# Four of the eight up chunks of three MLP rounds by seven products instead of eight

## The chip, the cores and the metric

The kernel runs on one core of a Trainium2 chip. The metric is the time of one execution on the device in microseconds (us). The kernel before was run three times: 1208.88 us in the median, 1205.19 the lowest and 1209.29 the highest. One further execution was recorded by the profiler, and everything that is read from the trace is from that one.

## What is computed

One inference step of two decoder layers, for a prompt of 512 tokens and eight samples of 8 tokens each, which share all weights: 576 tokens with 1024 features. Layer 0 mixes by retention and gated spatial mixing, layer 1 by windowed attention. After each mixer stands the MLP, and the MLP's first half is what the change touches:

```python
def sqrelu_mlp(h, w_up, w_down):
    return jnp.square(jax.nn.relu(h @ w_up)) @ w_down

hp = hp + sqrelu_mlp(rmsnorm(hp, norm_mlp[l]), mlp_w_up[l], mlp_w_down[l])
```

Here `h` has 1024 features, the hidden layer 4096. All is fp32. The kernel keeps that precision by splitting each operand of a product into a high part that the matrix engine takes in one pass (type fp32r) and the rest, the low part, and by adding three products: high by high, high by low, low by high.

## The kernel before

**Layout.** Activations lie with features on the 128 partitions and tokens along the free side. The residual is eight tiles `h[0]` to `h[7]` of 128 x 576. A matmul takes 288 tokens, one half of them. The normalised input of an MLP is eight pairs of tiles, `norm.xs[k]` = (high, low); the factor 1/rms (`norm.rv`) is multiplied in after the product.

**Rounds.** The hidden layer is worked off in four rounds of 1024 hidden features (`rounds_of`, `FB` = 8 chunks of 128 features a round). Each round has an up stage and a down stage.

The up stage runs four pairs of chunks. `up()` makes a chunk: 8 input blocks x 3 products x 2 token halves = 48 matmuls into two PSUM banks, the tile `acc`. VectorE then evacuates it, relu times 1/rms, into `t` (line 496), and ScalarE squares `t` into a quarter of the tile `q` (line 501). After both chunks of a pair, `combine` (lines 533 to 536, four VectorE operations of 288 columns) forms four sums and differences in `q`, and `two` splits seven blocks of `q` into the high tile `ahi` (ScalarE, line 504) and the low tile `alo` (VectorE, line 505), first three blocks (864 columns), then four (1152). `q` has one buffer.

The down stage multiplies these by the down weights, and it already works by seven products for eight (the scheme of Strassen and Winograd for 2 x 2 blocks: a pair of output chunks, two token halves, pairs of hidden chunks). `down_unit` does one of four such units in a round: products P1 to P7 of 12 matmuls each into PSUM banks (`product`, line 346), ScalarE copies of partial results from one bank to the next (`y`, `z`, `w`), and VectorE adding the results to `h` (line 557). The first unit of a round runs P1, P2, P3 and P5 for three of its four block rows first and then the fourth row of each, since the fourth needs the last pair of the up stage.

**Weights.** `order` lists all weight blocks of 512 KB in the order of use, and `jobs` the pieces in which they are split. An ordinary chunk has two pieces, `left` and `right`, of 512 columns; a unit has seven, of which four are of sums (`s1` to `s4`, VectorE, line 263, 512 columns each). `load_to` (line 235) issues the loads on SP's queue into `raw`, which has three buffers; the second weight of down units 1 and 3 is loaded into the place of `q` instead (the list `spare`). `prepare` and `split_low` split a piece: ScalarE casts the high part (line 278), VectorE subtracts it (line 289). High and low parts have six buffers each (`NW_`), so a piece can be split at most some five products ahead of its use.

**The order of work.** Inside `mlp`, VectorE and ScalarE take their instructions in the order in which the program writes them (`tc.manual_schedule`). `ahead_to(n)` writes the sums, casts and splits of the coming pieces at that place; it stands after every product and every chunk, ahead of the operations that evacuate that product's result. `raw` of a chunk comes free with the split of its `right` piece, of a unit's two weights with P2 and with P4.

## Time and profile before

| | us | share of the span |
|---|---|---|
| profiled execution | 1204.73 | |
| its span, first to last instruction | 1202.9 | 100% |
| TensorE matmul (PE) busy, 9130 instructions | 1182.9 | 98% |
| TensorE weight load (PEld) busy | 1164.8 | 97% |
| VectorE (DVE) busy, 1691 instructions | 908.2 | 76% |
| ScalarE (ACT) busy, 1111 instructions | 588.4 | 49% |
| GpSimd (POOL) busy | 148.3 | 12% |
| DMA, mean of the 16 engines | 91 GB/s | |

The granted TensorE clock is 0.997 of full speed over the span. A row of a timeline gives start, duration, engine, line, operation, what it writes and reads, and in brackets how long the engine stood idle before it and what ended that. Durations of neighbouring instructions overlap a little; the distance from start to start is what a queued instruction takes of its engine. In names, `t<-acc` writes `t` and reads `acc`.

### The profile page before, as it was taken

Reading aid. Unit: us, or ns where it says so; the run is one execution under the profiler, and the core shown is the slowest. Engines: PE = TensorE matmul, PEld = TensorE weight load, DVE = VectorE, ACT = ScalarE, POOL = GpSimd, SP = SyncE. Lnnn points to the kernel's source line nnn. Section 1 sums busy time; section 2 is a strip of 40 time slices with the busy share of each in tenths; the row PEclk is TensorE's granted clock in tenths of the full one; section 3 lists DMA queues with packets and bytes.
Section 4 is the critical chain, followed back from the end, with each engine's and each line's share of the span. In section 5 each row is a group of like instructions: output and inputs, shape, how many; then the busy total and the mean of one; then the engine's idle time right before and its main releaser. Section 6 shows DMA issues by size and latency. Waiting matters only on the chain.

```text
span 1202.9 us, 22619 instructions
## 1 busy us (share of the span) xinstructions
PE 1182.9 (98%) x9130; PEld 1164.8 (97%) x9130; DVE 908.2 (76%) x1691; ACT 588.4 (49%) x1111; POOL 148.3 (12%) x130
## 2 busy tenths in 40 slices
PE   8999999999999999999999999999999999999996
PEld 8899999999999999999999998999999999999996
DVE  8977797987866876885797787546785795795696
ACT  6333554654534444443466877445453453453452
POOL 4444250000000000000002653220000000000000
PEclk9999999999999999999999999999999999999999
DMA  7343222322332232242223211122233233233322
GB/s 269 110 142 112 88 65 80 88 81 78 90 106 87 77 117 71 71 120 75 88 87 111 72 53 55 53 76 71 84 105 89 71 106 91 68 106 88 87 73 79
DMA packets 38264, 109.43 MB, mean 91 GB/s; under 512 B 4160, under 2 KB 12544, under 8 KB 38144
## 3 DMA queue, kind: packets, MB, share of 16 engines
q1 hardware_dynamic: 37440, 107.36, 29.1%
q8 instruction: 72, 1.18, 0.4%
q10 hardware_dynamic: 720, 0.62, 0.2%
q14 instruction: 32, 0.26, 0.1%
HBM read 102.92 MB, written 6.03 MB: 91 GB/s over the span
## 4 chain that ended last, share of the span: by engine, by line
PE 82%; DVE 10%; ACT 4%; DMA 3%; issue 1%; SPq 0%; DVEq 0%; ACTq 0%
PE acc L334 50%; PE acc L346 10%; PE y L346 4%; PE f L346 4%; PE w L346 3%; PE z L346 3%; DVE wlo L289 3%; DMA raw<-in_w_dn 2%; ACT s L1158 1%; DVE alo L505 1%; PE tpp L1218 1%; DVE h L557 1%; ACT ahi L504 1%; PE dn L334 1%; PE op L1233 1%
## 5 line engine op out<-in xcount | busy, mean ns | idle before, releaser
L334 PE MATMUL acc<-xhi,whi 128*128 128x288 f32 x1504 | 321.7, 295 | 0.3 <-DVE vz L809 0.3
L334 PE MATMUL acc<-xhi,wlo 128*128 128x288 f32 x1504 | 319.2, 293 | 0.0
L334 PE MATMUL acc<-xlo,whi 128*128 128x288 f32 x1504 | 318.6, 293 | 0.0
L289 DVE TENSOR_TENSOR wlo<-raw,whi 128x512 fp32r<-128x512 f32 x317 | 235.7, 757 | 68.8 <-ACT whi L278 67.5
L334 PEld LDWEIGHTS acc<-xhi,whi 128*128 128x128 f32 x1504 | 239.5, 188 | 1.6 <-issue 1.1
L334 PEld LDWEIGHTS acc<-xhi,wlo 128*128 128x128 f32 x1504 | 240.5, 188 | 0.3
L334 PEld LDWEIGHTS acc<-xlo,whi 128*128 128x128 f32 x1504 | 240.1, 188 | 0.0
L278 ACT CAST whi<-raw 128x512 fp32r<-128x512 f32 x317 | 188.9, 619 | 100.5 <-PE acc L334 73.3
L501 ACT ACTIVATE q<-t 128x576 f32<-128x576 f32 x64 | 44.0, 687 | 227.8 <-DVE t L496 227.8
L278 ACT CAST whi<-s 128x512 fp32r<-128x512 f32 x140 | 83.4, 621 | 72.4 <-DVE s L263 62.8
L496 DVE SCALAR_TENSOR_TENSOR t<-acc,rstd 128x576 f32<-128x576 f32 x64 | 48.3, 755 | 80.6 <-PE acc L334 80.4
L289 DVE TENSOR_TENSOR wlo<-s,whi 128x512 fp32r<-128x512 f32 x140 | 95.9, 697 | 10.8 <-ACT whi L278 10.8
L505 DVE TENSOR_TENSOR alo<-q,ahi 128x864 fp32r<-128x864 f32 x64 | 77.2, 1205 | 8.3 <-ACT ahi L504 8.3
L504 ACT CAST ahi<-q 128x864 fp32r<-128x864 f32 x64 | 66.6, 1041 | 13.5 <-DVE q L536 12.5
L346 PE MATMUL acc<-ahi,wlo 128*128 128x288 f32 x340 | 71.4, 298 | 0.6
L346 PE MATMUL acc<-ahi,whi 128*128 128x288 f32 x340 | 71.4, 295 | 0.0
L346 PE MATMUL acc<-alo,whi 128*128 128x288 f32 x340 | 70.4, 295 | 0.0
L1102 POOL TENSOR_TENSOR kl<-z,kh 64x512 fp32r<-64x512 f32 x4 | 5.5, 1374 | 475.1 <-ACT kh L1099 474.9
L263 DVE TENSOR_TENSOR s<-raw 128x512 f32<-128x512 f32 x70 | 48.7, 695 | 19.8 <-DMA raw<-in_w_dn 19.8
L346 PEld LDWEIGHTS acc<-ahi,wlo 128*128 128x128 f32 x340 | 53.5, 188 | 2.5 <-DVE wlo L289 2.5
L346 PEld LDWEIGHTS acc<-ahi,whi 128*128 128x128 f32 x340 | 54.0, 188 | 0.0
L346 PEld LDWEIGHTS acc<-alo,whi 128*128 128x128 f32 x340 | 53.7, 188 | 0.0
(386 smaller groups left out, 2118.8 us busy)
## 6 DMA issues: line engine op xcount, KB each, us to landing
raw<-in_w_up SPq DMA_DIRECT2D x64, 512.0 KB
raw<-in_w_dn SPq DMA_DIRECT2D x64, 512.0 KB
raw<-in_w_in SPq DMA_DIRECT2D x22, 512.0 KB
raw<-in_w_o SPq DMA_DIRECT2D x16, 512.0 KB
raw<-in_w_qkv SPq DMA_DIRECT2D x10, 512.0 KB
h<-in_xT SPq DMA_DIRECT2D x8, 288.0 KB
s<-in_s SPq DMA_DIRECT2D x4, 512.0 KB
out_ret_s<-s SPq DMA_DIRECT2D x4, 512.0 KB
```

Of the source, the lines that this page charges most:

```text
L263: nc.vector.tensor_tensor(out=sums[k, i], in0=x, in1=b[y], op=ALU.add)
L278: nc.scalar.copy(out=hi, in_=src)
L289: nc.vector.tensor_tensor(out=lo, in0=src, in1=hi.bitcast(F32), op=ALU.subtract)
L334: nc.tensor.matmul(out, lhsT=w_, rhs=x_[:, hf if isinstance(hf, slice) else half(hf)], start=(start and si == 0), stop=(stop and si == 2))
L346: nc.tensor.matmul(out, lhsT=w[wi][:, k * P:(k + 1) * P], rhs=x(k)[xi], start=(start and n == 0), stop=(stop and n == len(steps) - 1), ski ...
L496: nc.vector.scalar_tensor_tensor(out=halves(t), in0=view, scalar=0.0, in1=norm.rv, op0=ALU.max, op1=ALU.mult)
L501: nc.scalar.activation(out=flat(q[:, seg]), in_=t, func=AF.Square)
L504: nc.scalar.copy(out=hi[:, s0 - 1:s1 - 1], in_=q[:, s0:s1])
L505: nc.vector.tensor_tensor(out=lo[:, s0 - 1:s1 - 1], in0=q[:, s0:s1], in1=hi.bitcast(F32)[:, s0 - 1:s1 - 1], op=ALU.subtract)
L557: nc.vector.tensor_tensor(out=row[:, cols_], in0=row[:, cols_], in1=src, op=op)
L1158: nc.scalar.activation(out=s[:, n, cut_:], in_=s[:, n, cut_:], func=AF.Exp, bias=nm[:, n:n + 1], accum_out=den[:, n:n + 1])
L1218: nc.tensor.transpose(out=tp[:, i * P:(i + 1) * P], in_=s[:, n, hf * P:(hf + 1) * P], identity=ident)
```

## The change

In rounds 1, 2 and 3 of each MLP, pairs 1 and 3 of the up chunks become a unit of seven products as in the down stage (`up_unit`). The 2 x 2 blocks are two hidden chunks, two token halves, and pairs of input blocks. The four mixed operands of the input (`mixed`, split in high and low) are made once, by `mix`, in round 0, which keeps its eight plain chunks. The result of each product chain stands in a bank of its own (`x`, `y`, `f`, `z`, `w`); ScalarE copies `x` to `y`, `x` to `z` and `z` to `w`, each ahead of the product that goes on in the copy, and `f` into `q`. VectorE adds `f` to `z` and to `x`, and scales each of the four quarters (relu, or minimum with 0 where the sign is turned, times 1/rms); ScalarE squares two quarters at a time.

The combination and split of a pair (`pending`) move: where a unit follows, to behind its P1 and the copy of `y`; elsewhere to the start of the next pair, and for the last pair of a round to the end of the up stage. The plain chunks write their evacuation straight into `q` and square it there, and take their input blocks in the order 0, 2, 4, 1, 3, 5, 6, 7. The up weights are laid out on the host so that a block of 512 KB holds the same numbers in the order that both uses share; there are as many loads of the same size. A scratch size for DMA is set to 4096 bytes.

```diff
--- before.py
+++ after.py
@@ -113,6 +113,7 @@
 NCOL = 59
 UNIT = ("P1", "P5", "P6", "P2", "P7", "P3", "P4")
 SUMS = {"P1": "s1", "P5": "s2", "P2": "s3", "P6": "s4"}
+MIX = ((0, 1), (1, 0), (2, 0), (3, 0))
 FIRST_UNIT = ("P1", "P2", "P3", "P5", "P6", "P4", "P7")
 
 
@@ -200,10 +201,19 @@
             if m % 2:
                 spare.append(len(order) - 1)
 
+    def in_units(r, p):
+
+        return r > 0 and p % 2 == 1
+
     def mlp_order(l, last):
         up, dn = a[f"w_up{l}"], a[f"w_dn{l}"]
         for r in range(32 // FB):
-            add_pieces([up[r * FB + f] for f in range(FB)])
+            for p in range(FB // 2):
+                pair = [up[r * FB // 2 + p, i] for i in range(2)]
+                if in_units(r, p):
+                    add_unit(pair, False)
+                else:
+                    add_pieces(pair)
             for m in range(KC // 2):
                 if last and r == 32 // FB - 1 and m == KC // 2 - 1:
                     add_pieces([dn[r, m, i] for i in range(2)])
@@ -469,52 +479,138 @@
 
     def rounds_of(norm, nxt, mp):
         rounds, closing = 32 // FB, Closing(COL["fin"])
+        operand = {"P1": 0, "P2": 2, "P3": 1, "P5": 3, "P6": 4, "P7": 5, "P4": 6}
+        mixed = []
 
         def up():
 
             acc, got = acc_tile(), take(2)
-            for k in range(KC):
-                block([acc[:, hf, 0:TH] for hf in range(2)], cut(got, k), norm.xs[k], (0, 1), k == 0, k == KC - 1)
+            for n, k in enumerate((0, 1, 2, 4, 5, 6, 3, 7)):
+
+                block([acc[:, hf, 0:TH] for hf in range(2)], cut(got, k), norm.xs[2 * (k % 4) + k // 4], (0, 1),
+                      n == 0, n == KC - 1)
             ahead_to(used[0] + NW_ - 2)
             return acc[:, :, 0:TH]
 
+        def mix(i, q):
+
+            a, b = 2 * i, 2 * i + 1
+            ga, gb = (cols[:, norm.gcol + c:norm.gcol + c + 1] for c in (a, b))
+            one, two_ = slice(TH, T), slice(0, TH)
+            t1, t3, u2, u4 = (q[:, n] for n in range(4, 8))
+            nc.scalar.activation(out=t3, in_=h[a][:, two_], func=AF.Copy, scale=ga)
+            for out, src, g, in1, op in ((t1, h[a][:, one], ga, t3, ALU.subtract), (t3, h[b][:, two_], gb, t3, ALU.subtract),
+                                         (u2, h[b][:, two_], gb, t1, ALU.add), (u4, h[b][:, one], gb, u2, ALU.subtract)):
+                nc.vector.scalar_tensor_tensor(out=out, in0=src, scalar=g, in1=in1, op0=ALU.mult, op1=op)
+            his, los = [], []
+            for src, sign in ((q[:, 4:6], 1.0), (q[:, 6:8], -1.0)):
+                hi, lo = (ks("xn", F32R) if i % 2 else mp.tile([P, T], F32R, name="xn", tag="xn", bufs=8) for _ in range(2))
+                nc.scalar.activation(out=halves(hi), in_=src, func=AF.Copy, scale=sign)
+                nc.vector.scalar_tensor_tensor(out=halves(lo), in0=src, scalar=sign, in1=halves(hi.bitcast(F32)),
+                                               op0=ALU.mult, op1=ALU.subtract)
+                for mine, t in ((his, hi), (los, lo)):
+                    mine.extend(halves(t)[:, n] for n in range(2))
+            his, los = ([v[n] for n in (0, 2, 1, 3)] for v in (his, los))
+            parts_ = []
+            for part, mine in zip(range(2), (his, los)):
+                xa, xb = norm.xs[a][part], norm.xs[b][part]
+                parts_.append([xa[:, one], xb[:, two_], xb[:, one]] + mine)
+            mixed.append(parts_)
+
+        def up_unit(last_pair):
+
+            x = acc_tile()[:, 0, 0:TH]
+
+            def run(n, out, start, ahead=NW_ - 1):
+                product(out, take(1)[0], lambda k: [t[operand[n]] for t in mixed[k]], range(4), start, True, True)
+                if ahead:
+                    ahead_to(used[0] + ahead)
+
+            def copied(name, src):
+                out = m_tile(name)[:, 0:TH]
+                nc.scalar.copy(out=out, in_=src)
+                ahead_to(used[0] + NW_ - 1)
+                return out
+
+            def scaled(seg, src, op):
+                nc.vector.scalar_tensor_tensor(out=q[:, seg], in0=src, scalar=0.0, in1=norm.rv[:, seg % 2],
+                                               op0=op, op1=ALU.mult)
+
+            run("P1", x, True, 0)
+            y = m_tile("y")[:, 0:TH]
+            nc.scalar.copy(out=y, in_=x)
+            last_pair()
+            q = q_tile()
+            ahead_to(used[0] + NW_ - 1)
+            f = m_tile("f")[:, 0:TH]
+            run("P5", f, True)
+            run("P6", x, False, 0)
+            z = copied("z", x)
+
+            nc.scalar.copy(out=q[:, 3], in_=f)
+            run("P2", y, False)
+            scaled(1, y, ALU.max)
+            run("P7", z, False, 0)
+            w_ = copied("w", z)
+
+            nc.vector.tensor_tensor(out=q[:, 2], in0=z, in1=q[:, 3], op=ALU.add)
+            scaled(2, q[:, 2], ALU.min)
+            run("P3", x, False)
+            nc.vector.tensor_tensor(out=q[:, 0], in0=x, in1=q[:, 3], op=ALU.add)
+            scaled(0, q[:, 0], ALU.max)
+            nc.scalar.activation(out=flat(q[:, 0:2]), in_=flat(q[:, 0:2]), func=AF.Square)
+            run("P4", w_, False)
+            scaled(3, w_, ALU.min)
+            nc.scalar.activation(out=flat(q[:, 2:4]), in_=flat(q[:, 2:4]), func=AF.Square)
+            return q
+
+        def q_tile():
+
+            return mp.tile([P, 8, TH], F32, name="q", tag="q", bufs=1)
+
         def flat(v):
             return v.rearrange("p a b -> p (a b)")
 
+        pending = lambda: None
         for r in range(rounds):
             acts, firsts = [], []
             for p in range(FB // 2):
-
-                q = mp.tile([P, 8, TH], F32, name="q", tag="q", bufs=1)
-                hi = mp.tile([P, 7, TH], F32R, name="ahi", tag="ahi", bufs=FB // 2)
-                lo = mp.tile([P, 7, TH], F32R, name="alo", tag="alo", bufs=FB // 2)
-                for j in range(2):
+                if in_units(r, p):
+                    q = up_unit(pending)
+                else:
+                    pending()
+                    q = q_tile()
+                for j in range(0 if in_units(r, p) else 2):
                     view = up()
                     if r == 0 and p == 0 and j == 0:
                         norm.finish()
-                    t = mp.tile([P, T], F32, name="t", tag="t")
-                    nc.vector.scalar_tensor_tensor(out=halves(t), in0=view, scalar=0.0, in1=norm.rv,
+                    seg = slice(2 * j, 2 * j + 2)
+                    nc.vector.scalar_tensor_tensor(out=q[:, seg], in0=view, scalar=0.0, in1=norm.rv,
                                                    op0=ALU.max, op1=ALU.mult)
                     if p == FB // 2 - 1 and j == 1:
                         ahead_to(used[0] + NW_ - 1)
-                    seg = slice(2 * j, 2 * j + 2)
-                    nc.scalar.activation(out=flat(q[:, seg]), in_=t, func=AF.Square)
-
-                def two(s0, s1):
-                    nc.scalar.copy(out=hi[:, s0 - 1:s1 - 1], in_=q[:, s0:s1])
-                    nc.vector.tensor_tensor(out=lo[:, s0 - 1:s1 - 1], in0=q[:, s0:s1],
-                                            in1=hi.bitcast(F32)[:, s0 - 1:s1 - 1], op=ALU.subtract)
-
-                b12 = q[:, 0]
-                combine(*(q[:, i] for i in range(8)))
-                two(1, 4)
-                two(4, 8)
-                acts.append([[t_[:, i] for i in range(7)] for t_ in (hi, lo)])
-                if nxt is None and r == rounds - 1:
-
-                    bh, bl = (mp.tile([P, TH], F32R, name=n, tag=n, bufs=FB // 2) for n in ("b12h", "b12l"))
-                    split_into(b12, bh, bl)
-                    firsts.append((bh, bl))
+                    nc.scalar.activation(out=flat(q[:, seg]), in_=flat(q[:, seg]), func=AF.Square)
+                    if r == 0 and (p, j) in MIX:
+                        mix(MIX.index((p, j)), q)
+
+                def pending(q=q, acts=acts, firsts=firsts, r=r):
+
+                    hi = mp.tile([P, 7, TH], F32R, name="ahi", tag="ahi", bufs=FB // 2)
+                    lo = mp.tile([P, 7, TH], F32R, name="alo", tag="alo", bufs=FB // 2)
+                    combine(*(q[:, i] for i in range(8)))
+                    for seg in (slice(0, 3), slice(3, 7)):
+                        src = q[:, seg.start + 1:seg.stop + 1]
+                        nc.scalar.copy(out=hi[:, seg], in_=src)
+                        nc.vector.tensor_tensor(out=lo[:, seg], in0=src, in1=hi.bitcast(F32)[:, seg], op=ALU.subtract)
+                    acts.append([[t_[:, i] for i in range(7)] for t_ in (hi, lo)])
+                    if nxt is None and r == rounds - 1:
+
+                        bh, bl = (mp.tile([P, TH], F32R, name=n, tag=n, bufs=FB // 2) for n in ("b12h", "b12l"))
+                        split_into(q[:, 0], bh, bl)
+                        firsts.append((bh, bl))
+
+            pending()
+            pending = lambda: None
             between = []
             spare_open[0] = True
             for m in range(KC // 2):
@@ -1412,6 +1508,10 @@
         r = len(w) // D
         return w.reshape(r, 4, 2, P, 4, 2, P).transpose(0, 4, 5, 3, 2, 1, 6).reshape(r, 4, 2, P, 8, P)
 
+    def up(w):
+
+        return w.reshape(4, 2, P, 16, 2, P).transpose(3, 4, 2, 1, 0, 5).reshape(16, 2, P, 8, P)
+
     def cols(v):
         return v.reshape(-1, P).T
 
@@ -1447,14 +1547,14 @@
         "rot": ROT,
     }
     for l in range(2):
-        out[f"w_up{l}"] = chunks(i["mlp_w_up"][l])
+        out[f"w_up{l}"] = up(i["mlp_w_up"][l])
         out[f"w_dn{l}"] = down(i["mlp_w_down"][l])
     return {k: np.ascontiguousarray(v) for k, v in out.items()}
 
 
 def kernel(**inputs):
     arrays = layouts({k: np.asarray(v) for k, v in inputs.items()})
-    nc = bacc.Bacc("TRN2", target_bir_lowering=False, num_devices=1)
+    nc = bacc.Bacc("TRN2", target_bir_lowering=False, num_devices=1, dynamic_dma_scratch_size=4096)
     a = {k: nc.dram_tensor("in_" + k, v.shape, F32, kind="ExternalInput").ap() for k, v in arrays.items()}
     o = {k: nc.dram_tensor("out_" + k, s, F32, kind="ExternalOutput").ap() for k, s in OUTS.items()}
     with tile.TileContext(nc) as tc:
```

## The prediction

> **What bounds the kernel now.** I read the page's first part, then a table by stage, then the chain of waits that ended last, then the VectorE, ScalarE and TensorE timelines around the end of one round.
>
> ```profile
> span 1202.9 us, 22619 instructions
> PE 1182.9 (98%) x9130; PEld 1164.8 (97%) x9130; DVE 908.2 (76%) x1691; ACT 588.4 (49%) x1111; POOL 148.3 (12%) x130
> ```
>
> TensorE (PE) is busy nearly all the time. That is an average, so the next view takes one round of the first MLP apart: its up stage, then its down stage.
>
> ```profile
> 350.00:400.00 50.00, 50.00 (x387) 50.00 (x386) 29.26 (x46) 19.47 (x29) 0.00 (x0) 1.00 0.27 83
> 400.00:445.00 45.00, 44.92 (x337) 44.49 (x336) 39.61 (x74) 22.90 (x42) 0.00 (x0) 1.00 0.34 96
> ```
>
> The columns after the stretch are its length, then PE, weight loads, VectorE (DVE), ScalarE (ACT), GpSimd. PE is full in both stages at granted clock 1.00. DVE is 59% busy in the up stage and 88% in the down stage: the up stage has the spare DVE time, and there the change works.
>
> ```profile
> 350.01 49.93 PE acc L334 x384
> 405.62 3.51 DMA raw<-in_w_dn
> 414.80 1.59 PE acc L346 x12
> 416.39 1.60 PE y L346 x12
> ...
> 445.05 49.93 PE acc L334 x384
> ```
>
> These rows of the chain give PE's prices. An up stage of 8 chunks is 384 matmuls in 49.93 us, so a pair of chunks (96) takes 12.48 us. A product of a down unit (12 matmuls) takes 1.593 us (414.80 to 416.39), a round 95.0 (350.01 to 445.05). The DMA row shows that each round hangs on something besides PE: a weight load issued at 405.62. The next fence is DVE from the last two pairs of this up stage into the down stage.
>
> ```profile
> 387.49 0.76 DVE L496 SCALAR_TENSOR_TENSOR t<-acc,rstd 128x576 f32<-128x576 f32 x1 [1.07 <-PE acc L334]
> 388.16 0.45 DVE L533 TENSOR_TENSOR q<-q 128x288 f32<-128x288 f32 x1
> 389.00 0.46 DVE L534 SCALAR_TENSOR_TENSOR q<-q 128x288 f32<-128x288 f32 x1 [0.39 <-ACT q L501]
> ...
> 391.42 1.36 DVE L505 TENSOR_TENSOR alo<-q,ahi 128x1152 fp32r<-128x1152 f32 x1 [0.26 <-ACT ahi L504]
> 392.70 0.69 DVE L263 TENSOR_TENSOR s<-raw 128x512 f32<-128x512 f32 x1
> 393.30 1.29 DVE L289 TENSOR_TENSOR wlo<-raw,whi 128x512 fp32r<-128x512 f32 x2
> 394.50 1.41 DVE L263 TENSOR_TENSOR s<-s,raw 128x512 f32<-128x512 f32 x2
> 395.83 0.75 DVE L496 SCALAR_TENSOR_TENSOR t<-acc,rstd 128x576 f32<-128x576 f32 x1
> 397.91 1.29 DVE L289 TENSOR_TENSOR wlo<-s,whi 128x512 fp32r<-128x512 f32 x2 [1.32 <-ACT whi L278]
> 399.97 0.76 DVE L496 SCALAR_TENSOR_TENSOR t<-acc,rstd 128x576 f32<-128x576 f32 x1 [0.77 <-PE acc L334]
> 400.64 0.68 DVE L289 TENSOR_TENSOR wlo<-s,whi 128x512 fp32r<-128x512 f32 x1
> ...
> 402.17 0.45 DVE L535 TENSOR_TENSOR q<-q 128x288 f32<-128x288 f32 x1
> 402.54 0.46 DVE L536 SCALAR_TENSOR_TENSOR q<-q 128x288 f32<-128x288 f32 x1
> ...
> 404.23 1.36 DVE L505 TENSOR_TENSOR alo<-q,ahi 128x1152 fp32r<-128x1152 f32 x1 [0.27 <-ACT ahi L504]
> ...
> 409.15 0.69 DVE L263 TENSOR_TENSOR s<-raw 128x512 f32<-128x512 f32 x1 [1.43 <-DMA raw<-in_w_dn]
> ```
>
> Three things are to be seen. First, DVE works in program order: the evacuation at 395.83 comes with no idle time before it, behind sums and splits. Second, the round's last combination and split end at 405.59 (404.23 + 1.36). PE begins the down stage at 399.77 and reaches the matmul that needs them at 405.87:
>
> ```profile
> 399.77 0.55 PE L346 MATMUL acc<-ahi,whi 128*128 128x288 f32 x3
> 405.87 0.29 PE L346 MATMUL f<-alo,whi 128*128 128x288 f32 x1
> ```
>
> So the cover is 0.28 us. Third, that same end frees the buffer q, in which the second weight of down unit 1 lands (issue 405.62), and DVE stands still for it until 409.15, 3.53 us after the issue. The chain from the last up evacuation through this split and this load is therefore as long as PE's own work: whatever comes later at 405.59 makes the round later by as much.
>
> **The change, part by part.** *Products.* In rounds 1 to 3 pairs 1 and 3 become units of seven products: 7 x 1.593 = 11.15 us for 12.48, so 1.33 us less PE work in each of 12 units, 15.9 us in all.
>
> *DVE work of a unit.* Start-to-start distances are the price of queued instructions: 0.60 us for 512 columns (392.70 to 393.30), 0.67 for an evacuation of 576 (387.49 to 388.16), 0.37 for 288 (402.17 to 402.54). A pair of chunks has 4 splits and 2 evacuations: 3.74 us. A unit has 7 splits, 4 sums and 6 instructions of 288 (four scalings, two additions): 11 x 0.60 + 6 x 0.37 = 8.82. Combination and split of the activations are common to both. So DVE gains 5.1 us of work a unit, while PE gives it 1.33 us less time. The four operations of 288 that read PSUM are not in the trace as such; between half of the 576 row (0.34) and a 288 row (0.37) I take the latter.
>
> [...]
>
> *The end of a round.* The second unit (pair 3) must be followed at once by the down stage. I count DVE's queue from the evacuation of the chunk before the pair (387.49) to the end of the last split (405.59): 18.10 us now. Afterwards:
> - that evacuation, combination and split of pair 2: 387.49 to 392.70, 5.21 us, as now;
> - eight splits of weights (P7, P3, P4 of the unit and five ahead for the down stage; the six weight buffers allow none earlier) and the four sums for down unit 0: 12 x 0.60 = 7.2;
> - six operations of 288: 2.2;
> - a new wait. After P3 ScalarE squares two halves, then casts the weight for P6 of the down unit, and that weight's split stands in DVE's queue ahead of the scaling of P4's result. DVE waits out the square and the cast, 1.3 us by the rows below (0.69 + 0.62). Queued behind it are the scaling, the combination and both splits;
> - from the second square to the end of the split as now: 388.28 to 392.78, 4.50, and 0.1 before it.
>
> Sum 20.5 us, 2.4 more than now. ScalarE's rows for this are:
>
> ```profile
> 388.28 0.69 ACT L501 ACTIVATE q<-t 128x576 f32<-128x576 f32 x1 [4.29 <-DVE t L496]
> ...
> 397.27 1.65 ACT L278 CAST whi<-s 128x512 fp32r<-128x512 f32 x3
> ...
> 405.14 0.38 ACT L573 COPY acc<-acc 128x288 f32<-128x288 f32 x1 [0.94 <-PE acc L346]
> 405.43 0.62 ACT L278 CAST whi<-raw 128x512 fp32r<-128x512 f32 x1
> ```
>
> *Late entry.* The unit of pair 1 loads DVE the same way: 5.21, eight splits, two sums, six of 288 and the wait. Its first sum for pair 3 needs that unit's second weight. There are three buffers, so this load cannot be issued before the second half of pair 2's first weight is split, 5.2 + 5 x 0.60 = 8.2 us after the evacuation that precedes unit 1; it lands 3.5 later, at 11.7. DVE asks at 8.2 + 0.60 + 3 x 0.37 = 9.9 and waits up to 1.8. From there its chain ends as that of unit 3: 11.7 + 0.6 (sum) + 0.6 (split) + 0.74 + 1.3 + 0.6 + 0.37 + 4.6 = 20.5. Pair 2 still asks DVE for a sum, a split and an evacuation (22.4), then ScalarE for a square and two casts (0.69 + 2 x 0.55) and DVE for the last split: 24.8. PE's end of pair 2 asks for the next evacuation at 11.15 + 12.48 = 23.6. So unit 3 would begin 1.2 us late; without the wait of 1.8 it begins on time. Between 0 and 1.2, the difference of two sums of twenty rows, I take the middle, 0.6.
>
> *What stays covered.* ScalarE's four new copies (0.29 each by 405.14 to 405.43), among them z ahead of P7: it is queued behind both activation casts and three weight casts, so it ends about 5.9 us into the unit, and P7 begins at 6.4. With the late entry, P7 of the second unit waits 0.1 to 0.7; this lies in DVE's shadow and adds nothing to the chain above. Nothing is added to SP's queue: as many loads of 512 KB as before, in the same order; the smaller scratch and the new block order in the chunks remove and add no instruction, and I cost them at 0.
>
> *Per round.* Gain of the first unit 1.33 (PE is not held there); the second unit's gain is lost, since DVE's chain ends later than PE. So +2.4 + 0.6 - 1.33 = +1.7 us, with ends +1.1 and +2.3. Six rounds: +10 (6.5 to 14).
>
> *Round 0.* It keeps its chunks and gains four mixes. One mix is four DVE operations of 288 and two of 576, 4 x 0.37 + 2 x 0.67 = 2.8, with waits for ScalarE's square, copy and casts of some 1.1. The last lies between the evacuations at 395.83 and 399.97, where DVE idles 1.32 + 0.77 = 2.1. About 1.8 sticks out if none of the waits overlap, 0 if they fall into the idle time; I take 0.9 in each MLP, 2 us in all.
>
> **Sum.** The profiled execution took 1204.73 us (span 1202.9 and 1.8 around it): +12 gives 1217. It lies 4.2 under the median of the three runs, 1208.88, and 0.5 under the lowest, 1205.19; I add half of the first, 2, and say 1219.
>
> **Rivals.** *The gain arrives (faster).* PE is the bound, its work falls by 15.9, and DVE's lateness is taken up by weights split up to five products ahead. For it: the down stage already runs DVE at 88% and loses PE 0.08 us in 45; the up stage has 20 us of idle DVE. Against it: weights ahead do not help the activations, whose split is last in the queue. All of 15.9 (1189, or 1193 against the median) needs the chain of unit 3 within 18.10 - 1.33 = 16.8 us, less than the 17.5 that are left of the 20.5 without its waits (0.39, 0.26, 1.3, 0.1, 0.69, 0.27), so hardly; a chain of 18.1 gives 1.33 a round, 8 us, 1197 to 1201. The sign turns at 19.4. Chance 0.2. [...]
>
> *It evens out.* A chain of 19.4, for instance when no late entry comes and the cast for P6 is done before P4 ends (1.1 us less): 1205 to 1215. Chance 0.22.
>
> *More waits (slower still).* The z copy is held up in every unit and PE stalls ahead of P7, 0.7 x 12 = 8 us on top, where the first unit's gain would go too: 1227. Within the slower cases; chance 0.1, beside 0.48 for the forecast.
>
> **How the numbers follow.** Runs of this kernel spread by 0.3%, so 0.5% (6 us) is about what can be told from no change. Faster by more than that 0.2, within it 0.22, slower 0.58. The forecast is 1219; its own ends are 1211 (no late entry, mix hidden) and 1226. The range reaches down to 1197, a part of the faster case, and up to 1230 for the stalls at P7. What it leaves out is the full gain and a loss of over 1.8%, under 0.2.
>
> **What would show it.** In the profile after: 9130 - 144 = 8986 matmuls; the first unit's stretch of a round near 11.2 us with PE full; DVE over 95% busy in the second unit's stretch; PE idle for 2 to 4 us at the fourth block of down unit 0, released by alo; rounds 1 to 3 longer by 1 to 2.3 us than 95.0. Wrong it would be if the last alo of a round ends within 19 us of the evacuation ahead of unit 3, or if PE has no gap at the start of the down stages, and rounds are 92 to 94 us.

## The result and the profile after

The changed kernel takes 1255.51 us in the median of four runs (1253.08 to 1256.39), the kernel before 1207.72 (1205.19 to 1209.29). The ratio is 1.0395, with an interval of 1.0369 to 1.042: about 48 us slower, where the forecast said 12. The profiled execution took 1253.08 us. Its page begins:

```profile
span 1251.0 us, 22594 instructions
PE 1191.1 (95%) x8986; PEld 1165.9 (93%) x8986; DVE 995.9 (80%) x1871; ACT 634.6 (51%) x1219; POOL 148.2 (12%) x130
```

The 144 matmuls are gone, and still PE is busy 8.2 us longer than before: part of its work ran at a lower clock (0.983 of full speed over the span for 0.997 before), as the rows below show. VectorE got 88 us of work more. The page's chain of work that ended last says where the time is (the first line sums it up by engine):

```profile
PE 57%; DVE 24%; ACT 12%; issue 4%; DMA 3%; SPq 0%; POOL 0%; DVEq 0%; ACTq 0%; POOLq 0%
```

Before, PE had 82% of this chain, VectorE 10% and ScalarE 4%. PE is still the engine with most to do, but it is no longer what sets the end. The same chain in the window of the second round of the first MLP:

```profile
359.31 12.48 PE acc L344 x96
371.79 1.62 PE acc L356 x12
373.81 1.92 ACT ahi L603 x2
...
380.15 4.40 DMA raw<-in_w_up
...
413.78 0.69 DVE wlo L299
414.87 0.69 ACT q L564
416.79 0.98 DVE alo L604
417.81 0.85 PE acc L356 x2
```

The chain is on PE for the first pair and the first product of the unit, then it goes over to casts, a load and VectorE's splits, and comes back to PE only in the down stage. The table by stage (columns as before) has the up stage, the down stage, and a stretch of the latter:

```profile
359.15:408.69 49.54, 48.21 (x363) 47.66 (x362) 37.07 (x62) 22.76 (x39) 0.00 (x0) 1.00 0.24 75
408.69:459.34 50.65, 47.54 (x338) 46.95 (x337) 42.02 (x81) 25.05 (x46) 0.00 (x0) 0.93 0.31 94
416.50:422.30 5.80, 5.58 (x22) 5.23 (x23) 4.69 (x8) 2.07 (x3) 0.00 (x0) 0.50 0.32 93
```

The up stage should have come down from 49.93 to 47.3 with two units; it is at 49.54, with 1.3 us in which PE stands. The down stage grew from some 45.1 to 50.65, and in 5.8 us of it the clock is at half. VectorE's timeline from the evacuation ahead of the second unit to the round's last split shows why (it answers to the rows from 387.49 to 405.59 of before):

```profile
397.99 0.75 DVE L588 SCALAR_TENSOR_TENSOR q<-acc,rstd 128x576 f32<-128x576 f32 x1
...
403.19 1.29 DVE L299 TENSOR_TENSOR wlo<-s,whi 128x512 fp32r<-128x512 f32 x2
...
409.50 0.69 DVE L299 TENSOR_TENSOR wlo<-s,whi 128x512 fp32r<-128x512 f32 x1 [0.32 <-ACT whi L288]
...
413.78 0.69 DVE L299 TENSOR_TENSOR wlo<-s,whi 128x512 fp32r<-128x512 f32 x1 [1.26 <-ACT whi L288]
414.39 0.45 DVE L536 SCALAR_TENSOR_TENSOR q<-w,rstd 128x288 f32<-128x288 f32 x1
414.76 0.45 DVE L629 TENSOR_TENSOR q<-q 128x288 f32<-128x288 f32 x1
...
418.00 1.36 DVE L604 TENSOR_TENSOR alo<-q,ahi 128x1152 fp32r<-128x1152 f32 x1 [0.25 <-ACT ahi L603]
```

From 397.99 to 419.36 (418.00 + 1.36) the chain takes 21.37 us; before it took 18.10. The new wait of the forecast is there: 1.26 us for a cast, with the scaling of P4's result and the whole combination queued behind it. PE's timeline across the same moment:

```profile
413.05 0.56 PE L356 MATMUL f<-ahi,wlo 128*128 128x288 f32 x3
416.55 0.61 PE L356 MATMUL acc<-ahi,whi 128*128 128x288 f32 x1 [2.94 <-ACT ahi L603]
416.95 0.44 PE L356 MATMUL y<-ahi,whi 128*128 128x288 f32 x1
417.19 0.44 PE L356 MATMUL g<-ahi,whi 128*128 128x288 f32 x1
```

PE has no work left at 413.6 and stands 2.94 us. Then its matmuls start 0.24 us apart (416.95 to 417.19) instead of 0.13, the half clock of the table.

I measure a round from its first up matmul to that of the next round. A round 0 is measured from the first up matmul behind those of the norm, and the last round ends with the first matmul of the final norm. By rounds 0 to 3 of both MLPs the whole difference is found:

| us | round 0 | 1 | 2 | 3 | round 0 | 1 | 2 | 3 |
|---|---|---|---|---|---|---|---|---|
| before | 88.50 | 95.03 | 95.17 | 95.38 | 88.89 | 95.06 | 94.81 | 92.26 |
| after | 97.92 | 100.19 | 99.74 | 100.15 | 98.03 | 99.80 | 99.67 | 98.32 |

The six rounds with units lose 30.2 us, 5.0 each, where the forecast had 1.7. The two rounds 0, which have no unit, lose 18.6, where it had 2. Round 1 of the first MLP splits so: from its start to the evacuation ahead of the last pair 37.64 before (349.85 to 387.49) and 38.84 now, +1.20; the chain to the end of the last split +3.27; from there to the end +0.69, to which the half clock belongs. In the other seven rounds the stretch behind the last split differs from before by -0.1 to +0.5 us, so nearly all of the loss lies ahead of that split.

What round 0 does is seen on VectorE's timeline, here its evacuations and mixes:

```profile
268.09 0.75 DVE L588 SCALAR_TENSOR_TENSOR q<-acc,rstd 128x576 f32<-128x576 f32 x1
270.02 2.06 DVE L504 SCALAR_TENSOR_TENSOR q<-h,cols,q 128x288 f32<-128x288 f32 x4 [1.18 <-ACT q L501]
...
280.88 2.06 DVE L504 SCALAR_TENSOR_TENSOR q<-h,cols,q 128x288 f32<-128x288 f32 x4 [1.24 <-ACT q L501]
...
285.57 0.75 DVE L588 SCALAR_TENSOR_TENSOR q<-acc,rstd 128x576 f32<-128x576 f32 x1
...
291.97 0.75 DVE L588 SCALAR_TENSOR_TENSOR q<-acc,rstd 128x576 f32<-128x576 f32 x1
293.96 2.06 DVE L504 SCALAR_TENSOR_TENSOR q<-h,cols,q 128x288 f32<-128x288 f32 x4 [1.24 <-ACT q L501]
295.94 1.59 DVE L509 SCALAR_TENSOR_TENSOR xn<-q,xn 128x576 fp32r<-128x576 f32 x2
297.45 0.68 DVE L299 TENSOR_TENSOR wlo<-raw,whi 128x512 fp32r<-128x512 f32 x1
...
299.25 0.75 DVE L588 SCALAR_TENSOR_TENSOR q<-acc,rstd 128x576 f32<-128x576 f32 x1
...
314.25 0.75 DVE L588 SCALAR_TENSOR_TENSOR q<-acc,rstd 128x576 f32<-128x576 f32 x1
```

The mix behind 291.97 holds VectorE from 292.64 (0.67 after the evacuation) to 297.45, 4.81 us, of which 1.24 is a wait for ScalarE. From 285.57 to 299.25 a pair takes 13.68 us of VectorE's queue, and PE needs 12.48 for it. The second evacuations of pairs 0, 1 and 3 are the rows at 268.09, 285.57 and 314.25. In the kernel before they stood here:

```profile
268.22 0.75 DVE L496 SCALAR_TENSOR_TENSOR t<-acc,rstd 128x576 f32<-128x576 f32 x1
...
279.28 0.76 DVE L496 SCALAR_TENSOR_TENSOR t<-acc,rstd 128x576 f32<-128x576 f32 x1 [1.27 <-PE acc L334]
...
304.88 0.76 DVE L496 SCALAR_TENSOR_TENSOR t<-acc,rstd 128x576 f32<-128x576 f32 x1 [1.09 <-PE acc L334]
```

So VectorE is on time at the end of pair 0 and 6.3 us late at the end of pair 1. Between those two rows stand two mixes, of chunks (0, 1) and (1, 0). At the end of pair 3 it is 9.4 us late. Before, the last split ended 5.82 us after the start of the down stage; now it ends 13.2 us after it, and PE waits:

```profile
312.90 0.90 PE L356 MATMUL g<-ahi,whi 128*128 128x288 f32 x3 [3.03 <-ACT whi L288]
```

This wait is for a cast that stands on ScalarE behind the casts of the last mix. For the last split itself PE waits another 0.81 us, at 318.30.

### The profile page after: what moved, and what is told of

The parts are those of the page before. It is cut to its first block, busy times and chain, and to the rows that moved or that the text cites. A ratio compares the mean times of both kernels' runs of the same rounds, so it can differ in the third digit from the quotient of the medians.

```text
span 1251.0 us, 22594 instructions
## 1 busy us (share of the span) xinstructions
PE 1191.1 (95%) x8986; PEld 1165.9 (93%) x8986; DVE 995.9 (80%) x1871; ACT 634.6 (51%) x1219; POOL 148.2 (12%) x130
## 4 chain that ended last, share of the span: by engine, by line
PE 57%; DVE 24%; ACT 12%; issue 4%; DMA 3%; SPq 0%; POOL 0%; DVEq 0%; ACTq 0%; POOLq 0%
PE acc L344 23%; PE acc L356 12%; DVE wlo L299 8%; PE w L356 4%; PE z L356 4%; PE f L356 4%; PE y L356 3%; ACT ahi L603 3%; ACT whi L288 3%; DMA raw<-in_w_up 2%; DVE alo L604 2%; DVE s L273 2%; DVE q L588 2%; ACT q L592 1%; DVE q L504 1%
## 5 line engine op out<-in xcount | busy, mean ns | idle before, releaser
L344 PE MATMUL acc<-xhi,whi 128*128 128x288 f32 x1120 | 242.0, 297 | 2.5 <-DVE q L588 2.0
L344 PE MATMUL acc<-xhi,wlo 128*128 128x288 f32 x1120 | 239.2, 295 | 0.0
L344 PE MATMUL acc<-xlo,whi 128*128 128x288 f32 x1120 | 238.5, 294 | 0.0
L344 PEld LDWEIGHTS acc<-xhi,whi 128*128 128x128 f32 x1120 | 178.6, 188 | 4.8 <-issue 4.3
L344 PEld LDWEIGHTS acc<-xhi,wlo 128*128 128x128 f32 x1120 | 179.9, 188 | 0.3
L344 PEld LDWEIGHTS acc<-xlo,whi 128*128 128x128 f32 x1120 | 179.5, 188 | 0.0
L288 ACT CAST whi<-s 128x512 fp32r<-128x512 f32 x188 | 112.0, 618 | 91.5 <-DVE s L273 77.1
L299 DVE TENSOR_TENSOR wlo<-s,whi 128x512 fp32r<-128x512 f32 x188 | 127.6, 690 | 18.8 <-ACT whi L288 18.8
L356 PEld LDWEIGHTS acc<-ahi,whi 128*128 128x128 f32 x340 | 56.4, 198 | 20.5 <-ACT ahi L603 19.1
L273 DVE TENSOR_TENSOR s<-s,raw 128x512 f32<-128x512 f32 x94 | 64.7, 688 | 0.3
L588 DVE SCALAR_TENSOR_TENSOR q<-acc,rstd 128x576 f32<-128x576 f32 x40 | 30.1, 754 | 35.3 <-PE acc L344 35.1
```

What stands on the lines that cost most here:

```text
L273: nc.vector.tensor_tensor(out=sums[k, i], in0=x, in1=b[y], op=ALU.add)
L288: nc.scalar.copy(out=hi, in_=src)
L299: nc.vector.tensor_tensor(out=lo, in0=src, in1=hi.bitcast(F32), op=ALU.subtract)
L344: nc.tensor.matmul(out, lhsT=w_, rhs=x_[:, hf if isinstance(hf, slice) else half(hf)], start=(start and si == 0), stop=(stop and si == 2))
L356: nc.tensor.matmul(out, lhsT=w[wi][:, k * P:(k + 1) * P], rhs=x(k)[xi], start=(start and n == 0), stop=(stop and n == len(steps) - 1), ski ...
L588: nc.vector.scalar_tensor_tensor(out=q[:, seg], in0=view, scalar=0.0, in1=norm.rv, op0=ALU.max, op1=ALU.mult)
```

## The experiments

My theory after this result (A): VectorE's queue, in program order, sets the end of a round. Mixes overfill it in round 0, and a unit as the last pair puts the last combination behind a whole unit's splits. The first rival (B): units and mixes cost what they cost wherever they stand. The second (C), for which the 4.40 us of the load speak: loads and casts set the pace, not VectorE. Each run is compared with runs of the kernel before on the same chip.

**Mixes alone.** No pair becomes a unit; the mixed operands are made and not used.

```diff
     def in_units(r, p):
-        return r > 0 and p % 2 == 1
+        return False
```

> The four mixes of round 0 are made but no unit uses them: all chunks are plain. Theory A (VectorE's queue is the bound: the mixes overfill it in round 0, and the unit of pair 3 puts the last combination of a round late): round 0 of each MLP stays 9 us longer, the other rounds return to 95.0 us, so 1207.7 + 18 = 1226 us. Theory B (the mixes are covered by idle VectorE time and the units cost wherever they stand): about 1209 us.

Measured: 1224.01 us, ratio 1.0154 (1.0134 to 1.0174), 18.8 us slower. Rounds 0 take 98.28 and 98.11, as in the changed kernel, and the others 94.97, 94.88, 95.31 in the first MLP, as before. So the mixes alone cost all that round 0 loses, and nothing else. This run also has the new block order, the new layout of the up weights, the smaller scratch and the combination moved to the next pair, so none of these costs anything that shows in a round.

**Units alone.** The mixed operands are replaced by plain ones.

```diff
                     if r == 0 and (p, j) in MIX:
-                        mix(MIX.index((p, j)), q)
+                        a_, b_ = (norm.xs[2 * MIX.index((p, j)) + c] for c in range(2))
+                        mixed.append([[xa[:, TH:T], xb[:, 0:TH], ...] for xa, xb in zip(a_, b_)])
```

> Units as in the changed kernel, but the mixes are left out and the products take unmixed blocks of the same size in their place (the result is not the reference's). Theory A: round 0 back at the time of before, rounds 1 to 3 as in the changed kernel: 1255.5 - 18 = 1237 us. Theory B: about 1254 us.

Measured: 1236.97 us, ratio 1.0261 (1.023 to 1.0293), 31.7 us slower. Round 0 of the first MLP is back at 88.40, the other three take 101.41, 99.64 and 101.04, and the last split ends 10.7 us after the start of the down stage, as in the changed kernel. The two halves, 18.8 and 31.7, add up to the whole within the spread: they are separate causes.

**Units at pairs 0 and 2.** The same amount of work; a plain pair stands last.

```diff
-        return r > 0 and p % 2 == 1
+        return r > 0 and p % 2 == 0
```

> The two units of a round stand at pairs 0 and 2, so that the last pair is plain again; mixes as in the changed kernel. Theory A: the last combination comes 18 to 19 us after the evacuation ahead of the last pair, the units gain 2 x 1.33 us less some 0.6 a round: rounds near 93 us, 1207.7 + 18 - 12 = 1214 us. Theory B: the place does not matter, 1250 to 1256 us.

Measured: 1231.07 us, ratio 1.0207 (1.0186 to 1.0227). The six rounds lose 7.7 us together instead of 30.2, so the place matters, against B; but they should have gained. The last split still ends 8.0 us after the start of the down stage. VectorE's timeline in the second unit has the reason:

```profile
392.10 0.46 DVE L536 SCALAR_TENSOR_TENSOR q<-q,rstd 128x288 f32<-128x288 f32 x1
394.96 0.69 DVE L273 TENSOR_TENSOR s<-raw 128x512 f32<-128x512 f32 x1 [2.40 <-DMA raw<-in_w_dn]
```

A sum for a later unit stands in the queue before its weight has come, and VectorE waits 2.40 us with the unit's scalings and the combination queued behind it. It is the kind of wait from which the forecast had its "late entry", larger than I took it.

**The scaling of P4 first.** In the unit, sums, casts and splits written behind P4 are moved behind the scaling and the square of its result.

```diff
-            run("P4", w_, False)
+            run("P4", w_, False, 0)
             scaled(3, w_, ALU.min)
             nc.scalar.activation(out=flat(q[:, 2:4]), in_=flat(q[:, 2:4]), func=AF.Square)
+            ahead_to(used[0] + NW_ - 1)
```

> Only the order behind P4 of a unit is changed: its result is scaled and squared ahead of the next weight's cast and split. Theory A: the wait of 1.3 us and the split of 0.6 leave the chain to the last combination, 1.9 us in each of six rounds and perhaps 0.5 more by a shorter PE gap: 1255.5 - 11 to 15, so 1240 to 1244 us. Theory B: no change, 1254 to 1256 us.

Measured: 1250.11 us, ratio 1.0375 (1.0352 to 1.0399), a miss. VectorE's timeline:

```profile
411.93 0.45 DVE L536 SCALAR_TENSOR_TENSOR q<-w,rstd 128x288 f32<-128x288 f32 x1
413.85 0.69 DVE L299 TENSOR_TENSOR wlo<-s,whi 128x512 fp32r<-128x512 f32 x1 [1.47 <-ACT whi L288]
414.45 0.45 DVE L630 TENSOR_TENSOR q<-q 128x288 f32<-128x288 f32 x1
```

The scaling comes some 2 us earlier (3.76 us after the start of the down stage instead of 5.70), but the cast and its split still stand ahead of the combination, so the wait only changed its place: 1.47 us instead of 1.26, and the last split ends 10.55 us after the start of the down stage instead of 10.67. To be rid of it, the split would have to go behind the combination. That was not tried.

**Sums on GpSimd.** If VectorE is short of time, the sums of the weights could go to an idle engine; in the kernel before the same edit should then cost nothing.

```diff
-nc.vector.tensor_tensor(out=sums[k, i], in0=x, in1=b[y], op=ALU.add)
+nc.gpsimd.tensor_tensor(out=sums[k, i], in0=x, in1=b[y], op=ALU.add)
```

In the changed kernel:

> The changed kernel with all sums of weights (s1 to s4) added on GpSimd instead of VectorE; nothing else. Theory A (VectorE's queue sets the end of each round): unit 3 enters on time, since VectorE no longer waits for the load in a sum (2.3 us) and has 2.4 us less to do in each unit, and the chain to the last combination loses 2.4 us: rounds 1 to 3 near 95 us for 99.9, round 0 2.4 us shorter: 1255.5 - 30 - 5 = 1220 us. Theory C (the loads into three buffers and ScalarE's casts set the pace, VectorE only shows it): a sum on GpSimd takes longer than 0.6 us and delays the casts behind it, so 1255 us or more.

In the kernel before:

> The kernel before with all sums on GpSimd. Theory A: VectorE has idle time in the up stages there and the last combination follows PE, so nothing but the short standstill for a load behind it changes: 1203 to 1206 us beside 1205. Theory C: as A or slower.

Measured: 1266.63 us, ratio 1.0512 (1.0496 to 1.0529), and 1215.44, ratio 1.0085 (1.0069 to 1.0101). Both slower. By its number the first speaks for C, but the second shows that the edit has a price of its own. GpSimd's and VectorE's timelines in it, the same stretch of a down stage:

```profile
412.94 1.37 POOL L263 TENSOR_TENSOR s<-raw 128x512 f32<-128x512 f32 x1 [18.74 <-DMA raw<-in_w_dn]
414.38 3.32 POOL L263 TENSOR_TENSOR s<-s,raw 128x512 f32<-128x512 f32 x2
```

```profile
412.46 0.69 DVE L289 TENSOR_TENSOR wlo<-s,whi 128x512 fp32r<-128x512 f32 x1 [1.20 <-ACT whi L278]
...
414.99 1.56 DVE L289 TENSOR_TENSOR wlo<-s,whi 128x512 fp32r<-128x512 f32 x1
416.48 0.44 DVE L557 TENSOR_TENSOR h<-h,w 128x288 f32<-128x288 f32 x1
```

A split takes 0.69 us at 412.46, of which a sum overlaps the last 0.2, and 1.56 at 414.99, beside sums all along. So VectorE gives back a good part of what it is spared: its 457 splits of weights take 400.8 us instead of 331.6 in the kernel before, with 140 sums less to do, which took 97.3 there. The two runs don't decide between A and C.

**A lighter version, sums on GpSimd.** Pairs 0 and 2, sums on GpSimd, and a mix that does ScalarE's copy and VectorE's four operations ahead of the chunk's evacuation and leaves the low parts for behind it.

```diff
-        return r > 0 and p % 2 == 1
+        return r > 0 and p % 2 == 0
...
                     view = up()
+                    rest = mix(MIX.index((p, j)), q) if r == 0 and (p, j) in MIX else lambda: None
...
-                        mix(MIX.index((p, j)), q)
+                    rest()
```

> Units at pairs 0 and 2, sums on GpSimd, and the mixes of round 0 written so that VectorE does not wait for ScalarE in them (the ScalarE copy and the four VectorE operations ahead of the chunk's evacuation, the two low parts behind it). Theory A: VectorE's work then fits beside PE in every stage: round 0 within 1 us of before, the others 95.0 - 2.66 + 0.5 = 92.9 us, so 1205 - 13 + 2 = 1194 us. Theory B (units cost wherever they stand): 1215 us or more.

Measured: 1225.01 us, ratio 1.0162 (1.0144 to 1.018), a miss: the expectation had left out what a sum on GpSimd costs VectorE. Round 0 of the second MLP is down to 93.25 from 98.03: writing part of the mix ahead helps.

**One unit, at pair 1 or at pair 3.** This is the cleanest test of A against B: the same unit at two places, without mixes.

```diff
-        return r > 0 and p % 2 == 1
+        return r > 0 and p == 1
```

> One unit a round, at pair 1, with two plain pairs behind it; no mixes, unmixed blocks in their place (not the reference's result). Theory A (VectorE's queue): the two plain pairs give it back its lateness, the last combination stands as before, and PE's 1.33 us a round are kept: rounds 93.7 us, 1205.2 - 8 = 1197 us. Theory B (a unit costs wherever it stands): no gain, 1205 to 1215 us.

```diff
-        return r > 0 and p % 2 == 1
+        return r > 0 and p == 3
```

> One unit a round, at pair 3, entered on time; no mixes, unmixed blocks in their place (not the reference's result). Theory A: the last combination comes some 21.4 us after the evacuation ahead of the unit instead of 18.1, PE's gain is lost in that: rounds 98.3 us, 1205.2 + 20 = 1225 us. Theory B: as the kernel with one unit at pair 1.

Measured: 1202.14 us, ratio 0.9965 (0.995 to 0.9979), and 1229.4, ratio 1.019 (1.017 to 1.021). One unit a round gains 4.0 us in all at pair 1 and loses 23.2 at pair 3; B is out. At pair 1 the last split ends 5.81 us after the start of the down stage, as before, and at pair 3 10.44. The table by stage of the run with pair 1 (a round's up stage and down stage):

```profile
351.32:400.54 49.22, 49.22 (x374) 49.22 (x373) 34.97 (x58) 22.32 (x36) 0.00 (x0) 1.00 0.29 86
400.54:445.66 45.12, 45.04 (x338) 44.59 (x337) 38.11 (x72) 22.86 (x42) 0.00 (x0) 1.00 0.31 94
```

PE is full in both stages. The up stage is shorter by 0.7, not by 1.33. The chain of this round says where the rest is:

```profile
351.49 12.48 PE acc L344 x96
...
375.11 25.61 PE acc L344 x192
```

The pair ahead of the unit takes 12.48 us, the two pairs behind it 25.61, 0.65 more than twice that, with PE busy and at full clock. Why two of those matmuls take 0.267 us instead of 0.260 is not settled. It is not a matter of the units alone: in round 0 of the first MLP of the kernel before, two matmuls take 0.267 us too (PE rows at 284.94 to 286.81, granted clock 1.00).

**Sums one job later.** The late entry by itself: a sum is written no more than one piece ahead of the pieces to be split, instead of two. One run has the changed kernel with this edit alone; the other has it with the units at pairs 0 and 2, the lighter mix, the scaling first, and sums on VectorE.

```diff
-while summed[0] < min(len(parts) + 2, len(jobs)):
+while summed[0] < min(len(parts) + 1, len(jobs)):
```

> The changed kernel with the sums of weights written one job later in VectorE's queue; nothing else. If the wait of 2.3 us for a load in the first sum of unit 3 makes its late entry, it goes and rounds 1 to 3 fall by about 2 us: 1255.5 - 12 = 1243 us. If the late entry comes from the amount of work alone: 1253 to 1256 us.

Measured: 1244.05 us, ratio 1.0311 (1.0295 to 1.0328). In round 1 the evacuation ahead of the last pair comes 36.75 us after the start of the round instead of 38.84:

```profile
385.22 0.69 DVE L273 TENSOR_TENSOR s<-raw 128x512 f32<-128x512 f32 x1 [0.95 <-DMA raw<-in_w_up]
...
396.42 0.75 DVE L588 SCALAR_TENSOR_TENSOR q<-acc,rstd 128x576 f32<-128x576 f32 x1
```

The round starts at 359.67 and its last split ends at 417.79, so the chain from that evacuation is 21.37 us, the same to the hundredth. The edit took away the late entry, 2.1 us in this round, and left the chain. The wait for the load is 0.95 us instead of 2.29, and a wait of 0.66 for a cast behind it is gone. The six rounds together are only 6.6 us shorter, and round 3 of the first MLP is 1.8 longer. So the 1243 of the expectation was met in part by chance, by gains that lie outside these rounds.

> Units at pairs 0 and 2, mixes written so that VectorE does not wait for ScalarE in them, sums of weights one job later in the queue (so that VectorE is not held by a load while it has other work), results of P4 scaled ahead of the next split; all sums on VectorE. Theory A: round 0 some 3 us over before (the last pair still has a mix and four sums), other rounds 94 to 95 us: 1205.2 + 6 - 3 = 1202 to 1212 us. If the lateness is not in VectorE's queue, as with units at pairs 0 and 2 alone: 1228 us or more.

Measured: 1200.28 us (1199.38 to 1201.8), ratio 0.995 (0.9934 to 0.9966), a little better than expected and faster than both kernels. Round 1 by stage:

```profile
355.10:402.65 47.55, 47.55 (x362) 47.55 (x361) 36.76 (x63) 24.33 (x43) 0.00 (x0) 1.00 0.30 98
402.65:448.16 45.51, 45.30 (x338) 44.60 (x337) 42.16 (x80) 23.10 (x43) 0.00 (x0) 1.00 0.26 84
```

With the same seven products for eight in the same number of pairs, PE is full through the up stage, the last split ends 6.23 us after the start of the down stage, and PE stands 0.2 us. The six rounds gain 8.1 us of the 15.9 (three of them 2.0 each; why the others gain less was not followed up); round 0 of the second MLP is still 2.5 us longer than before. Of C a part remains: VectorE's long waits are for a load and for casts. But the loads and casts are as many in this run, and the units no longer cost more than they gain, so what decides is where such a wait stands in VectorE's queue. Rounds 1 to 3 of this run differ from those with the units at pairs 0 and 2 alone by the later sums and the scaling first, and they went from a loss of 7.7 us to a gain of 8.1. Which of the four edits brought how much was not tried one by one, beyond the runs above.

**Mixes earlier.** The same kernel with the mixes in chunks (0, 0), (0, 1), (1, 0), (2, 0), to free the last pair of round 0.

```diff
-MIX = ((0, 1), (1, 0), (2, 0), (3, 0))
+MIX = ((0, 0), (0, 1), (1, 0), (2, 0))
```

> As e10_light_02, but the four mixes stand in chunks 0 and 1 of pair 0 and chunk 0 of pairs 1 and 2, so that the last pair of round 0 has none. Theory A: the last combination of round 0 comes 5.8 to 6.2 us after the down stage begins instead of 7.9, round 0 of each MLP loses 2 us more of its excess, the rest stays: 1200.3 - 4 = 1196 us. If the work of VectorE in pair 0 is too much (it also makes the factor 1/rms there): no better than 1200 us.

Measured: 1204.43 us, ratio 0.9989 (0.9978 to 0.9999), no better than 1200, as the second case of the expectation has it. In the first MLP the last split of round 0 ends 5.81 us after the start of the down stage, as before the change, but now pair 0 is overfull. PE's timeline, and the table for the stretch behind the gap:

```profile
284.64 0.50 PE L344 MATMUL acc<-xhi,whi 128*128 128x288 f32 x2 [1.96 <-ACT xn L508]
```

```profile
284.64:288.90 4.26, 4.25 (x21) 4.26 (x22) 3.88 (x8) 2.72 (x5) 0.00 (x0) 0.60 0.16 44
```

PE stands 1.96 us and then runs at 0.60 of its clock. The gain at the end of round 0 is spent at its beginning.

## Why the prediction was right in direction and wrong in size

*Products.* Right: 8986 matmuls, and the first unit's stretch is 11.1 us (371.63 to 382.76) with PE full, as said.

*The chain of the last unit.* The mechanism was right, the size short: 21.37 us, and the forecast was 20.5. Its parts agree at the beginning (5.20 for evacuation, combination and split; 5.21 forecast) and at the end (4.49 from the second square to the end of the split; 4.50), and the new wait is 1.26 for 1.3. What was missing lies between: 11.68 us from 403.19 to 414.87, where the forecast had 7.2 + 2.2 + 1.3 + 0.1 = 10.8. Of the missing 0.9, a second wait for a cast is 0.32 (the row at 409.50). The rest is spread over five places of the queue with some 0.1 us each; two of them are scalings that read the addition just ahead and start 0.48 and 0.49 us after it, where I had priced 0.37, from rows that wait for nothing.

*Late entry.* The step that failed is "Between 0 and 1.2, the difference of two sums of twenty rows, I take the middle, 0.6." On time the evacuation would have been at 395.81 (PE ends pair 2 at 395.61, and 0.2 passes as before); it came at 397.99, 2.2 us late. The load took 4.40 us, not 3.53, and VectorE waited 2.29 for it. So not even the full 1.2 would have been enough. The row of the wait is this:

```profile
384.58 0.69 DVE L273 TENSOR_TENSOR s<-raw 128x512 f32<-128x512 f32 x1 [2.29 <-DMA raw<-in_w_up]
```

The run with later sums shows that the place of this sum in the queue was the cause: written one piece later, it waits 0.95 us, and the evacuation comes 2.1 us earlier.

*Per round.* The gain of the first unit, -1.33, was kept, but 0.37 of it went in pair 2, which took 12.85 us instead of 12.48 (382.76 to 395.61). So 2.2 - 1.33 + 0.37 is the 1.20 to the evacuation, and with 3.27 the last split ends 4.5 us later; this and what is lost behind it are the 5.0 of a mean round. The forecast 1.7 left out 0.9 of the chain, 1.6 of the late entry, and 0.4 of a plain pair.

*Round 0.* The largest part of the miss: 18.6 us, where I had 2. The step that failed is "The last lies between the evacuations at 395.83 and 399.97, where DVE idles 1.32 + 0.77 = 2.1. [...] I take 0.9 in each MLP". The price of a mix was not far off, 4.81 for 3.9. But I weighed the last of the four alone, as if VectorE came to it on time. The pairs ahead have too little room as well. VectorE is 6.3 us late after pair 1, behind two mixes in a row. The next pair takes 13.68 us for 12.48, so the lateness is handed on and grows, the evacuations come late, and PE stands for a bank (0.69 us at 279.79, 0.65 at 300.15). The run with the mixes alone shows all of it.

*Covered work.* The copy of z held P7 of the last unit by 0.54 us, within the forecast 0.1 to 0.7. The copy of y held P6 by 0.79 us, a wait that the forecast did not have; the two are the 1.3 us in which PE stands in the up stage. Both lie in the shadow of VectorE's chain, whose parts above hold no wait for PE.

*What would show it.* PE's gap at the fourth block row of down unit 0 is there, 2.94 us for the forecast 2 to 4; it is put down to `ahi`, from the same combination. VectorE is busy 90% of the second unit's stretch (11.72 of 13.08 us), not over 95%: the rest is waits for ScalarE, 0.72, 0.39 and 0.22 us. The rounds are longer by 4.6 to 6.1, not by 1 to 2.3.

*The rivals.* The gain did not arrive, since the chain was 21.4 us, beyond the 19.4 at which the sign was to turn. "It evens out" needed no late entry and an early cast for P6; the entry was 2.2 us late and the cast was waited for. "More waits" had the right side and a wrong place: the waits were VectorE's own, not PE's ahead of P7.

## What to carry to other kernels

Where an engine works in program order, ask of each stage what stands in its queue ahead of the one result that the next stage waits for. Work that relieves a saturated engine at the price of a less busy one paid here only where such a result did not stand behind it: the same unit gains 4 us at one place and loses 23 at another. And price an addition that is made in several stretches in all of them in a row, with the lateness that each hands to the next. Lateness was given back here only by a later stretch with room of its own, as by the two plain pairs behind the unit at pair 1 (the last split 5.81 us after the start of the down stage, as before).

## What the runs showed of the hardware

**The clock after a short gap.** After gaps of 2.94 us (changed kernel) and 1.96 us (mixes earlier) the granted clock was 0.50 and 0.60 in the stretches behind them, for 5.8 and 4.3 us. In the changed kernel it cost little: 2.86 of the 5.8 us lie ahead of the end of the last split at 419.36, on which PE depends, and from there to the end of the round it is only 0.69 us more than before.

**GpSimd beside VectorE.** In the kernel before with its sums on GpSimd, two kinds of VectorE instruction part. A split took 0.68 us at 404.18, with GpSimd idle, and 1.56 at 414.99, beside a sum on GpSimd; in the mean the 140 splits of sums took 946 ns, for 697 in the kernel before. The additions of 288 columns, which read one of their inputs from PSUM, took 0.45 at 409.48, with GpSimd idle, and 0.44 at 416.48, beside a sum. No run shows what makes the difference.
